# One block layer on one core: pool half of the output projection spread into the attention, residual by way of DRAM, sums of squares on VectorE, mask of the maxima on TensorE

## The chip, the cores and the metric

The kernel runs on one core of a Trainium2 chip. The metric is the device time of one execution in microseconds. The kernel before takes 1159.4 us, the median of three runs (1159.33 to 1159.95). The engines are called as in the profile: PE (TensorE) with PEld for its weight loads, DVE (VectorE), ACT (ScalarE), POOL (GpSimd), and SP (SyncE), which issues most of the transfers; ACTq and SPq are the sequencers of those engines.

## The reference, cut to what matters

```python
def _layer(h, ...):                     # h: 16 meta tokens, then 1024 frames; 1024 channels
    n1 = _rmsnorm(h, norm1_w)
    q, k, v, fg, u = split(n1 @ w_in)   # 512, 512, 512, 8, 512
    q, k = _rmsnorm per head of 64      # 8 heads
    log_f = log_sigmoid(fg + b_fgate)
    a_out = _forgetting_attention(q, k, v, cumsum(log_f))
    pooled[g] = trailing mean of u[g] over 2, 4, 8, 16 rows, minus u[g]
    p_out = (pooled @ w_pool) * pool_scale
    h = h + concat([a_out, p_out]) @ w_out
    n2 = _rmsnorm(h, norm2_w)
    return h + (silu(n2 @ w_gate) * (n2 @ w_up)) @ w_down
```

The logit of query t and key s is q_t.k_s / 8 plus the sum of log f over s < j <= t, for s <= t; the softmax runs over s. All is float32, and the 16 meta rows are dropped at the end.

## The kernel before, in words

Everything lies transposed, with channels on the partitions. A float32 product is made of three matmuls: each operand is split into a high part of type fp32r and the remainder (xh and xl, wh and wl), and high x high, high x low and low x high are added up in PSUM. So each input needs a split, ACT writing the high part and DVE or POOL the low part, before PE can use it.

The order of the program is written out by hand, and every engine works through its own list in that order.

*Opening.* A loop over the 8 blocks of 128 channels (k) loads a block of h (xs), splits it (L187 on ACT, L188 on DVE), squares it (L200 on ACT), adds the square to sqacc (L201 on POOL), and runs 15 matmuls for the first keys and the forget gates. prep_v splits the weights of v (L157 to L160). Then comes v_mm(0), the first of nine 128-row pieces of v with 24 matmuls, and then the statistics: two kinds of small matmuls over the split of sqacc give the norm as a column and as a row (pc and qrow below stand for these; L258 to L273).

*Projections* of q, k and u follow, with the gates between the v pieces, then pool_map(g) for the four window groups (L482 to L486): pm on PE, its high part mph on ACT, its low part mpl on DVE.

*Output projection.* Its work is cut into jobs in the queue fill_q: out_job(x, b) is one block of 128 output channels (m) and one half of the sequence (b), either of the pool half (12 matmuls; 16 such jobs, open at once) or of the attention's heads 0 to 3 (6 matmuls; 16 jobs, open when head 3 is done). c_job does the same for heads 4 to 7 at the end. fill(n) runs the next n of them. The residual tile h2[m] is loaded from hT once and stays in SBUF; each job adds its PSUM result into it on DVE (L552).

*Attention.* stack(h) builds the operands of a head: ACT copies the high parts, SP moves them to the other half of the partitions (K<-K and Q<-Q, L598 to L605), and DVE makes the low parts (L609, L613); background(n) takes n pieces of this. For each of the 16 units (head h, half b) a first pass computes scores and their row maxima: mx_steps does two matmuls into a tile s, and DVE reduces it (L665), or, in the last chunk of each row, adds the causal mask maskB and reduces in one instruction (L662). mt turns the maxima into rows: DVE negates and splits them (L678, L679), its inner function fin has PE transpose them in four pieces and ACT copies the rows into Q2 (L684, L685). The second pass, sp_steps, computes the scores again with the maxima as two more rows of the contraction (st, L716 to L719: K1 with Q1, the mask, K2[:68] with Q2[:68]), takes the exponential on ACT, the low part pl on POOL or DVE (L736), and multiplies with v (pv). The maxima of later units are interleaved. FILL[u] is the share of a job that a step of unit u adds; whenever the sum passes one, a job from fill_q runs.

*Tail.* The norm before the feed-forward part, gate and up, and down, which are nearly all matmuls.

## Time and profile before

| | |
|---|---|
| median of three runs | 1159.4 us |
| the profiled execution | 1160.96 us, of which the span of its instructions is 1158.5 us |
| PE busy | 1120.6 us, 97% of the span |
| DVE, ACT, POOL busy | 762.3, 485.9 and 406.7 us |
| mean granted TensorE clock | 0.989 of full speed |
| chain of work that ended last | PE 80%, DVE 12%, ACT 3%, waiting for issue 3% |

The span runs from the first instruction to the last; 2.5 us of the execution lie outside it. Busy shares are means over stages that are bound by different things, so the groups of rows further down are cut by stage. A granted clock of 1.00 is 2.4 GHz, and 0.50 is 1.2 GHz.

### The profile page before, as it was taken

What the parts mean: (1) busy time and instruction counts of PE and PEld (TensorE: products, weight loads), DVE (VectorE), ACT (ScalarE), POOL (GpSimd) and SP (SyncE); (2) the same over time, 40 slices, a digit from 0 to 9 for tenths busy, and PEclk for the clock granted to TensorE, in tenths of its full rate; (3) what the DMA queues carried; (4) which work ended last, traced back from release to release, by engine and by line L of the source; (5) the groups of instructions that cost most, each with busy time, mean ns of one, the idle gap of its engine ahead of it and who ended that gap; (6) DMA issues with size and microseconds to landing.
All of it is one profiled execution on the core that took longest, in us unless ns stands there. A gap on an engine that the chain in (4) does not pass through costs nothing.

```text
span 1158.5 us, 14614 instructions
## 1 busy us (share of the span) xinstructions
PE 1120.6 (97%) x5251; PEld 921.4 (80%) x5251; DVE 762.3 (66%) x1230; ACT 485.9 (42%) x907; POOL 406.7 (35%) x336
## 2 busy tenths in 40 slices
PE   6899999999999999998999999999999999999998
PEld 5687999877868878776788888888888888888886
DVE  7524763685778886799654554455545569778985
ACT  7333431451768776534332332233123335343541
POOL 6200235251444665638544345334533510000000
PEclk9899999999999999999999999999999999999999
DMA  6201110251012113230323132213221379542452
GB/s 222 74 1 41 50 55 11 65 162 49 20 30 48 29 38 120 109 109 1 109 73 102 44 109 73 95 51 109 73 81 65 129 261 372 189 157 100 153 193 109
DMA packets 48407, 112.45 MB, mean 97 GB/s; under 512 B 6560, under 2 KB 9120, under 8 KB 48336
## 3 DMA queue, kind: packets, MB, share of 16 engines
q1 hardware_dynamic: 38512, 95.23, 25.3%
q10 hardware_dynamic: 9824, 16.30, 3.8%
q8 instruction: 41, 0.67, 0.2%
q14 instruction: 30, 0.25, 0.1%
HBM read 86.10 MB, written 19.92 MB: 92 GB/s over the span
## 4 chain that ended last, share of the span: by engine, by line
PE 80%; DVE 12%; ACT 3%; issue 3%; POOL 1%; DMA 0%; SPq 0%; ACTq 0%; DVEq 0%; POOLq 0%
PE gu L1125 11%; PE gu L1124 11%; PE gu L1123 10%; PE d L1365 6%; PE d L1364 6%; PE d L1363 6%; PE pj L402 3%; PE pj L403 3%; PE pj L401 3%; PE o L500 2%; PE o L501 2%; PE o L502 2%; PE v L240 2%; PE v L241 1%; PE v L242 1%
## 5 line engine op out<-in xcount | busy, mean ns | idle before, releaser
L1124 PE MATMUL gu<-cb,ws 128*128 128x512 f32 x560 | 221.3, 395 | 4.2 <-DVE ws L1114 4.1
L1125 PE MATMUL gu<-cb,ws 128*128 128x512 f32 x560 | 221.1, 395 | 0.0
L1123 PE MATMUL gu<-cb,ws 128*128 128x512 f32 x560 | 220.7, 394 | 0.0
L1114 DVE TENSOR_TENSOR ws<-wst,ws 128x512 fp32r<-128x512 f32 x120 | 97.2, 810 | 125.2 <-ACT ws L1113 125.2
L1124 PEld LDWEIGHTS gu<-cb,ws 128*128 128x128 f32 x560 | 105.5, 188 | 30.0 <-DVE ws L1114 5.1
L1113 ACT ACTIVATE ws<-wst 128x512 fp32r<-128x512 f32 x120 | 70.0, 621 | 137.7 <-POOL wst L1108 130.1
L1125 PEld LDWEIGHTS gu<-cb,ws 128*128 128x128 f32 x560 | 105.7, 189 | 24.4
L1123 PEld LDWEIGHTS gu<-cb,ws 128*128 128x128 f32 x560 | 105.4, 188 | 24.6
L1365 PE MATMUL d<-hd,wd 128*128 128x512 f32 x308 | 121.2, 394 | 0.0
L1364 PE MATMUL d<-hd,wd 128*128 128x512 f32 x308 | 121.2, 393 | 0.0
L1363 PE MATMUL d<-hd,wd 128*128 128x512 f32 x308 | 121.0, 393 | 0.0
L1137 POOL TENSOR_TENSOR e<-e,e 128x512 f32<-128x512 f32 x20 | 29.6, 1479 | 158.8 <-DVE e L1150 105.7
L736 POOL TENSOR_TENSOR pl<-p,ph 128x512 fp32r<-128x512 f32 (+4 forms) x58 | 64.6, 1126 | 47.2 <-ACT p L728 45.1
L402 PE MATMUL pj<-xh,wl 128*128 128x346 f32 (+2 forms) x216 | 72.9, 338 | 0.0
L401 PE MATMUL pj<-xh,wh 128*128 128x346 f32 (+2 forms) x216 | 72.9, 337 | 0.0
L403 PE MATMUL pj<-xl,wh 128*128 128x346 f32 (+2 forms) x216 | 72.9, 337 | 0.0
L1363 PEld LDWEIGHTS d<-hd,wd 128*128 128x128 f32 x308 | 57.9, 188 | 13.4
L1364 PEld LDWEIGHTS d<-hd,wd 128*128 128x128 f32 x308 | 57.9, 188 | 13.4
L1365 PEld LDWEIGHTS d<-hd,wd 128*128 128x128 f32 x308 | 57.8, 188 | 13.2
L293 POOL TENSOR_TENSOR s<-t,g 128x346 f32<-128x346 f32 (+2 forms) x20 | 21.6, 1084 | 131.8 <-ACT g L292 124.6
L1052 ACT ACTIVATE hd<-wst 128x512 fp32r<-128x512 f32 x77 | 48.0, 623 | 35.7 <-issue 26.9
L1053 DVE TENSOR_TENSOR hd<-wst,hd 128x512 fp32r<-128x512 f32 x77 | 52.7, 685 | 9.7 <-ACT hd L1052 9.7
(292 smaller groups left out, 2560.0 us busy)
## 6 DMA issues: line engine op xcount, KB each, us to landing
wst<-in_w_d SPq DMA_DIRECT2D x77, 256.0 KB, 3.1
wst<-in_w_g SPq DMA_DIRECT2D x22, 512.0 KB, 5.2
wst<-in_w_up SPq DMA_DIRECT2D x22, 512.0 KB, 3.7
wst<-hidd SPq DMA_DIRECT2D x22, 512.0 KB, 7.5
wst<-in_w_d SPq DMA_DIRECT2D x11, 512.0 KB, 4.5
hidd<-e ACTq DMA_DIRECT2D x20, 256.0 KB
h<-in_hT SPq DMA_DIRECT2D x8, 512.0 KB, 7.8
h2d<-h SPq DMA_DIRECT2D x16, 256.0 KB, 2.0
```

The costliest lines, as they stand in the source:

```text
L401: mm(p[:, :n], wh[:, W], xh[k][:, o:o + n], start=k == 0, stop=False)
L402: mm(p[:, :n], wl[:, W], xh[k][:, o:o + n], start=False, stop=False)
L403: mm(p[:, :n], wh[:, W], xl[k][:, o:o + n], start=False, stop=k == KT - 1)
L736: sub.tensor_tensor(pl[:sz, o0:o1], p32[:sz, o0:o1], f(ph)[:sz, o0:o1], op=OP.subtract)
L1113: A.activation(t[:, :512], src, AF.Copy)
L1114: E.tensor_tensor(t[:, 512:], src, f(t)[:, :512], op=OP.subtract)
L1123: mm(p, w[:, W], c[:, :512], start=k == 0, stop=False)
L1124: mm(p, w[:, Wl], c[:, :512], start=False, stop=False)
L1125: mm(p, w[:, W], c[:, 512:], start=False, stop=k == 3)
L1363: mm(p, w[:, W], h[:, LO], start=i == 0, stop=False)
L1364: mm(p, w[:, Wl], h[:, LO], start=False, stop=False)
L1365: mm(p, w[:, W], h[:, HI], start=False, stop=i == NPR - 1)
```

## The change

It does six things.

1. *Opening.* The squares are written in place over xs by ACT, one k later than before (square), and summed on DVE (sq_add): three of the sums inside the loop and four behind prep_v. POOL has no part in it. Three pieces of v stand ahead of the statistics where one did, and the gates start two pieces later.
2. *Mask of the maxima.* In the last chunk of each row PE adds the mask with one more matmul of 128 columns; DVE then does a plain reduction.
3. *Rows of maxima.* POOL negates and splits the maxima (three instructions of 128x4 per unit), PE transposes them in one piece to 8x128, ACT copies those into a small tile mr, and SP writes them into rows 66 and 67 of Q2 with two transfers.
4. *Residual.* Each job of the pool half loads its tile, and stores the result to DRAM (h2s, 8 stores of 512 KB); each job of the attention's first half loads it from there (8 loads of 512 KB).
5. *Where the jobs run.* Of the 16 pool jobs, 8 run before the first step of the second pass (RAMP = 2, then one, then five), and the rest in the units of the first heads by FILL. Before, all 16 ran there. FILL is 13/40 and 19/40 where it was 0, 11/40 and 14/40.
6. *Before the attention.* stack(0) stands ahead of pool_map, and its pieces and those of the last q norm (run_later) go between the pool groups.

```diff
 CHQ = ((16, 512), (528, 512))
 PRE = 1
 VC, VK = 640, 6
+SQ = 4
 RA, LW = 10, 4
 NB = (3, 6)
 CW, KW, SW, W1 = 2, 2, 3, 3
...
 MID = 1
 ND, DIRECT = 2, (1, 2, 3)
 AGE = 2
-FILL = [0] * 8 + [11 / 40] * 6 + [14 / 40] * 2
+RAMP = 2
+FILL = [13 / 40] * 8 + [19 / 40] * 8
 
 
 @with_exitstack
...
 
 
     table(6)
-    xh, xl = [], []
-    sqacc = None
+    xh, xl, sqs = [], [], []
+
+    def square(k):
+
+        A.activation(sqs[k], sqs[k], AF.Square)
+
+    def sq_add(k):
+        V.tensor_tensor(sqs[0], sqs[0], sqs[k], op=OP.add)
+
     wfs = const([128, KT, 16], FR, "wfs")
     fg_ps = [ps("fg") for _ in CH3]
     k0_ps = [ps("k0") for _ in CH3]
...
                 V.tensor_tensor(wfs[:, :, 8:16], wf3, f(wfs)[:, :, 0:8], op=OP.subtract)
         xh.append(h)
         xl.append(l)
+        sqs.append(xs)
         if k == 0:
             wk0_split(slice(128, 1024))
-            sqacc = ut(L, FT, "sqacc")
-            A.activation(sqacc, xs, AF.Square)
         else:
-            sq = ut(L, FT, "sq")
-            A.activation(sq, xs, AF.Square)
-            G.tensor_tensor(sqacc, sqacc, sq, op=OP.add)
+            square(k - 1)
+        if k >= 3 and k - 2 < SQ:
+            sq_add(k - 2)
         s0, s1 = k == 0, k == KT - 1
         W = slice(128 * k, 128 * k + 128)
         for c, (o, n) in enumerate(CH3):
...
 
     for i in range(KT - VK, 4):
         prep_v(i)
+    square(KT - 1)
+    for k in range(SQ, KT):
+        sq_add(k)
+    sqacc = sqs[0]
     fgT = ut(L, FT, "fgT")
     for c, (o, n) in enumerate(CH3):
         A.activation(fgT[:16, o:o + n], fg_ps[c][:16, :n], AF.Copy)
...
         sz = min(128, L - 128 * j)
         A.activation(v32[j // 2][:sz, 512 * (j % 2):512 * (j % 2) + 512], p[:sz], AF.Copy, scale=rcol[:sz, j:j + 1])
 
-    vp = v_mm(0)
+    v0, v1, vp = v_mm(0), v_mm(1), v_mm(2)
 
 
     acch, accl = split_w(sqacc, L, ut, A, V)
...
     k32[0] = ut(L, FT, "k32")
     for (o, n), p in zip(CH3, k0_ps):
         qk_evac(p, n, slice(o, o + n), kw, k32[0][:, o:o + n])
-    vn = v_mm(1)
-    v_evac(0, vp)
+    v_evac(0, v0)
+    v_evac(1, v1)
+    vn = v_mm(3)
+    v_evac(2, vp)
     vp = vn
     now, later[:] = later[:], []
     run_later(now)
...
         return load((w_u[i] if c == "u" else w_qk[2 * i + (c == "k")]).rearrange("p k f -> p (k f)"), 1024, aux)
 
     gt = gates()
-    for j in range(2, ST):
+    for j in range(4, ST):
         vn = v_mm(j)
         v_evac(j - 1, vp)
         vp = vn
-        if j % 2 == 0:
+        if j == 4:
+            now, later[:] = later[:], []
+            run_later(now)
+        if j != 8:
             next(gt, None)
-        if j == 2:
+        if j == 5:
             A.activation(rb, qrow, AF.Ln)
             A.activation(rb, rb, AF.Exp, scale=-0.5)
             rtm = ut(L, FT, "rtm")
...
             o += 128 * (k1 - k0)
         return s
 
+    h2s = [DR.tile([128, SEQ], FT, name=f"h2s{m}") for m in range(KT)]
+    hjob, hback = {}, []
+
     def h_load(x):
-        if x < len(jobs) and jobs[x][3] and h2[jobs[x][2]] is None:
-            h2[jobs[x][2]] = ut(SEQ, FT, "h2")
-            nc.sync.dma_start(h2[jobs[x][2]], hT[:, jobs[x][2], META:])
+        if x < len(jobs) and x not in hjob:
+            mix_of, ks, m, first = jobs[x]
+            hjob[x] = ut(SEQ, FT, "h2")
+            nc.sync.dma_start(hjob[x], hT[:, m, META:] if first else h2s[m])
+            if not first:
+                h2[m] = hjob[x]
+
+    def h_store():
+        for m, t in hback:
+            nc.sync.dma_start(h2s[m], t)
+        hback.clear()
 
     def out_split(s):
         n = s.shape[1]
...
                 if y < len(jobs) and y not in wo:
                     wo[y] = out_load(y)
             h_load(x)
+        else:
+            h_store()
             h_load(x + 1)
         p = out_mm(mix_of(), wo[x], b) if p is None else p
         S = slice(512 * b, 512 * b + 512)
-        V.tensor_tensor(h2[m][:, S], p, h2[m][:, S], op=OP.add)
+        V.tensor_tensor(hjob[x][:, S], p, hjob[x][:, S], op=OP.add)
         if b == 1:
             wo.pop(x)
+            if first:
+                hback.append((m, hjob[x]))
         elif x + 1 < len(jobs):
             wo[x + 1] = out_split(wo[x + 1])
 
...
 
     vd = ut(1024, FT, "vd").rearrange("p (i j c) -> p i j c", i=2, j=4)
     V.tensor_copy(vd[:, :, :, 64:128], onesf[:, None, 0:64].to_broadcast([128, 8, 64]).rearrange("p (i j) c -> p i j c", i=2))
-    Mc = [const([128, 4, 68], FR, f"Mc{i}") for i in range(2)]
-    for t in Mc:
-        G.memset(f(t), 0.0)
-        V.tensor_copy(t[:, :, 64:66], onesf[:, 0:8].rearrange("p (a e) -> p a e", e=2))
     heads = {}
 
     SE = V
...
                 def step(T=T, o=o, n=n, a=a, c=c, last=c == nch - 1):
                     p = ps("s")
                     mm(p[:, :n], Q1[:, T], K1[:, o:o + n], start=True, stop=False)
+                    if last:
+                        mm(p[:, n - 128:n], ident, maskB, start=False, stop=False)
                     mm(p[:, :n], Q2[0:66, T], K2[0:66, o:o + n], start=False, stop=True)
-                    if last:
-                        V.tensor_tensor_reduce(p[:, :n], p[:, :n], maskB[:, 512 - n:], 1.0, -3e38, OP.add, OP.max,
-                                               accum_out=mp[:, a, c:c + 1])
-                    else:
-                        V.tensor_reduce(mp[:, a, c:c + 1], p[:, :n], op=OP.max, axis=AX.X)
+                    V.tensor_reduce(mp[:, a, c:c + 1], p[:, :n], op=OP.max, axis=AX.X)
                 steps.append(step)
                 o += n
         return steps
 
-    mcount = [0]
-
     def mt(h, b):
         Q2 = heads[h][1]
-        mc = Mc[mcount[0] % 2]
-        mcount[0] += 1
-        mx = U.tile([128, 4], FT, tag="mx", bufs=3, name=nm("mx"))
+        mx, nm_, mc = [U.tile([128, c], dt, tag=s, bufs=3, name=nm(s)) for c, dt, s in ((4, FT, "mx"), (4, FT, "mn"), (8, FR, "mc"))]
         V.tensor_reduce(mx, mparts[h, b], op=OP.max, axis=AX.X)
-        V.tensor_scalar(mc[:, :, 66:67], mx[:, :, None], -1.0, None, op0=OP.mult)
-        V.scalar_tensor_tensor(mc[:, :, 67:68], mx[:, :, None], -1.0, f(mc)[:, :, 66:67], op0=OP.mult, op1=OP.subtract)
+        G.tensor_scalar(nm_, mx, -1.0, None, op0=OP.mult)
+        G.tensor_copy(mc[:, 0:4], nm_)
+        G.tensor_tensor(mc[:, 4:8], nm_, f(mc)[:, 0:4], op=OP.subtract)
 
         def fin():
             p = ps("mt")
-            for a in range(4):
-                nc.tensor.transpose(p.bitcast(FR)[:68, 128 * a:128 * a + 128], mc[:, a, :], ident)
-            A.activation(Q2[64:68, 512 * b:512 * b + 512], p[64:68], AF.Copy)
+            nc.tensor.transpose(p.bitcast(FR)[:8, :128], mc, ident)
+            mr = U.tile([8, 128], FR, tag="mr", bufs=3, name=nm("mr"))
+            A.activation(mr, p[:8, :128], AF.Copy)
+            for i in range(2):
+                nc.sync.dma_start(f(Q2)[66 + i:67 + i, 512 * b:512 * b + 512], f(mr)[4 * i:4 * i + 4])
         return fin
 
     a32 = {}
...
     wo[0] = out_split(wo0)
     h_load(0)
     wo[1] = out_load(1)
+    stack(0)
     for g in (3, 2, 1, 0):
         pool_map(g)
-    stack(0)
-    for x in range(2):
+        background(2)
+        if g in (2, 1):
+            now, later[:] = later[:], []
+            run_later(now)
+    background(99)
+    vsplit(0)
+    for x in range(RAMP):
         fill(1)
         background(3)
-        now, later[:] = later[:], []
-        run_later(now)
-    background(4)
-    vsplit(0)
-    for _ in range(7):
-        fill(1)
-        background(2)
+    background(99)
     stack(1)
     for s in mx_steps(*units[0]):
         s()
-        background(2)
+        background(1)
     fin = mt(*units[0])
-    fill(2)
+    fill(1)
+    background(99)
     fin()
 
     acc = [None, None]
```

**Order on DVE in the opening.** The names are xl (the low part of a block of h) and xs (the block, later its square; xs_121 gathers the sum). Before, from k = 2 to the first split of the weights of v:

```order
L188 SCALAR_TENSOR_TENSOR xl_181<-xs_178,n_97,xh_180 128x1040
L188 SCALAR_TENSOR_TENSOR xl_205<-xs_202,n_97,xh_204 128x1040
L188 SCALAR_TENSOR_TENSOR xl_236<-xs_233,n_97,xh_235 128x1040
L188 SCALAR_TENSOR_TENSOR xl_260<-xs_257,n_97,xh_259 128x1040
L188 SCALAR_TENSOR_TENSOR xl_284<-xs_281,n_97,xh_283 128x1040
L159 CAST wh_307<-wst_305 128x384
L160 TENSOR_TENSOR wl_308<-wst_305,wh_307 128x1024
```

After, the same stretch:

```order
L199 SCALAR_TENSOR_TENSOR xl_179<-xs_176,n_99,xh_178 128x1040
L199 SCALAR_TENSOR_TENSOR xl_201<-xs_198,n_99,xh_200 128x1040
L158 TENSOR_TENSOR xs_121<-xs_121,xs_154 128x1040
L199 SCALAR_TENSOR_TENSOR xl_231<-xs_228,n_99,xh_230 128x1040
L158 TENSOR_TENSOR xs_121<-xs_121,xs_176 128x1040
L199 SCALAR_TENSOR_TENSOR xl_254<-xs_251,n_99,xh_253 128x1040
L158 TENSOR_TENSOR xs_121<-xs_121,xs_198 128x1040
L199 SCALAR_TENSOR_TENSOR xl_277<-xs_274,n_99,xh_276 128x1040
L170 CAST wh_298<-wst_296 128x384
L171 TENSOR_TENSOR wl_299<-wst_296,wh_298 128x1024
```

Three additions have come in between the splits; the seven that POOL did in parallel (rows sqacc<-sqacc,sq of L201) are gone from its list.

**Order on DVE between pool_map and the first maxima.** mpl are the low parts of the pool groups (the last two belong to group 0), t, s, g and q the norm of the last q block, Q and K the low parts of head 0, h the addition of a job. Before:

```order
L486 SCALAR_TENSOR_TENSOR mpl_2001<-pm_2002,psc,mph_2000 128x512
L486 SCALAR_TENSOR_TENSOR mpl_2001<-pm_2008,psc,mph_2000 128x512
L552 TENSOR_TENSOR h_331_1954<-o_2018,h_331_1954 128x512
L290 SCALAR_TENSOR_TENSOR t_2048<-qrow_398,ss_2045 128x512
L290 SCALAR_TENSOR_TENSOR t_2058<-qrow_398,ss_2055 128x512
L552 TENSOR_TENSOR h_331_1954<-o_2065,h_331_1954 128x512
L609 TENSOR_TENSOR Q_354_2036<-q_124_777,Q_353_2035 64x512
L296 SCALAR_TENSOR_TENSOR s_360_2050<-s_360_2050,g_2049 128x512
L297 SCALAR_TENSOR_TENSOR g_2049<-s_360_2050,g_2049 128x512
L298 SCALAR_TENSOR_TENSOR q_300_1832<-pj_1848,qw,g_2049 128x512
L296 SCALAR_TENSOR_TENSOR s_364_2060<-s_364_2060,g_2059 128x512
L297 SCALAR_TENSOR_TENSOR g_2059<-s_364_2060,g_2059 128x512
```

After, from the third group on:

```order
L505 SCALAR_TENSOR_TENSOR mpl_2015<-pm_2016,psc,mph_2014 128x512
L505 SCALAR_TENSOR_TENSOR mpl_2015<-pm_2022,psc,mph_2014 128x512
L639 TENSOR_TENSOR Q_331_1969<-q_117_780,Q_330_1968 64x512
L310 SCALAR_TENSOR_TENSOR s_341_1999<-s_341_1999,g_1998 128x512
L311 SCALAR_TENSOR_TENSOR g_1998<-s_341_1999,g_1998 128x512
L312 SCALAR_TENSOR_TENSOR q_293_1826<-pj_1842,qw,g_1998 128x512
L310 SCALAR_TENSOR_TENSOR s_345_2009<-s_345_2009,g_2008 128x512
L311 SCALAR_TENSOR_TENSOR g_2008<-s_345_2009,g_2008 128x512
L312 SCALAR_TENSOR_TENSOR q_293_1826<-pj_1843,qw,g_2008 128x512
L505 SCALAR_TENSOR_TENSOR mpl_2038<-pm_2039,psc,mph_2037 128x512
L505 SCALAR_TENSOR_TENSOR mpl_2038<-pm_2045,psc,mph_2037 128x512
L643 TENSOR_TENSOR K_332_1970<-k_68_484,K_332_1970 64x520
```

The last two mpl have moved from ahead of the norm to behind all of its six instructions; two t (not shown) stand ahead of group 1.

**Order on SP around the operands of head 6.** Q<-kat and K<-kat fetch gate rows, K<-K and Q<-Q are the moves of stack(6), wos is a weight of an output job. Before:

```order
L514 DMA wos_3691<-in_w_out 128x256
L592 DMA Q_748_3787<-kat_642 2x1024
L593 DMA K_750_3789<-kat_642 4x1040
L598 DMA K_750_3789<-K_749_3788 64x520 x2
L605 DMA Q_747_3786<-Q_747_3786 64x512 x2
L514 DMA wos_3909<-in_w_out 128x256
```

After; h2s is a store of a residual tile, h<-h2s a load of one, and Q<-mr the two rows of maxima that unit (5, 1) needs:

```order
L533 DMA wos_3802<-in_w_out 128x256
L622 DMA Q_777_3876<-kat_665 2x1024
L623 DMA K_779_3878<-kat_665 4x1040
L628 DMA K_779_3878<-K_778_3877 64x520 x2
L550 DMA h2s_1934<-h_541_2912 128x1024
L544 DMA h_780_3886<-h2s_1928 128x1024
L635 DMA Q_776_3875<-Q_776_3875 64x512 x2
L712 DMA Q_699_3567<-mr_3916 1x4x128 x2
L533 DMA wos_3951<-in_w_out 128x256
```

The rows of unit (5, 1) are queued behind the store, the load and the moves of the head to come.

## Rows read from the trace of the kernel before

**Rows 1.** Page, busy time and share of each engine

```profile
PE 1120.6 (97%) x5251; PEld 921.4 (80%) x5251; DVE 762.3 (66%) x1230; ACT 485.9 (42%) x907; POOL 406.7 (35%) x336
```

**Rows 2.** Windows: stretch, length, busy time per engine, granted clock, DMA share, GB/s

```profile
5.80:37.50 31.70, 23.60 (x120) 17.70 (x121) 29.48 (x19) 18.86 (x21) 21.56 (x7) 0.95 0.52 185
34.60:41.00 6.40, 5.37 (x15) 4.15 (x16) 5.59 (x9) 2.71 (x5) 0.00 (x0) 0.50 0.62 184
228.00:261.30 33.30, 32.07 (x140) 25.51 (x138) 26.06 (x38) 18.29 (x37) 16.10 (x15) 1.00 0.53 160
284.70:463.50 178.80, 168.83 (x962) 139.87 (x960) 140.21 (x320) 131.06 (x292) 96.76 (x113) 0.98 0.17 46
290.30:293.60 3.30, 3.30 (x11) 2.52 (x10) 0.63 (x2) 2.57 (x7) 0.51 (x2) 0.50 0.00 0
443.90:447.20 3.30, 3.30 (x9) 2.52 (x9) 0.69 (x1) 2.87 (x6) 3.30 (x4) 0.50 0.88 288
```

**Rows 3.** Timeline of DVE in the opening: start, length, instruction

```profile
10.24 1.30 DVE L188 SCALAR_TENSOR_TENSOR xl<-xs,n,xh 128x1040 fp32r<-128x1040 f32 x1 [0.92 <-ACT xh L187]
12.26 16.28 DVE L188 SCALAR_TENSOR_TENSOR xl<-xs,n,xh 128x1040 fp32r<-128x1040 f32 x5 [0.72 <-ACT xh L187]
40.94 1.24 DVE L128 TENSOR_TENSOR wl<-sqacc,wh 128x1040 fp32r<-128x1040 f32 x1 [0.50 <-ACT wh L125]
```

**Rows 4.** Groups of POOL, 0 to 40 us: count, busy and mean, idle before

```profile
L201 POOL TENSOR_TENSOR sqacc<-sqacc,sq 128x1040 f32<-128x1040 f32 x7 | 21.6, 3080 | 8.3 <-ACT sq L200 7.8
```

**Rows 5.** Timeline of PE in the opening, around the end of the loop

```profile
25.63 0.32 PE L209 MATMUL k<-xl,wh 128*128 128x346 f32 x1
25.79 0.32 PE L210 MATMUL fg<-xl,wfs 128*16 128x346 f32 x1
...
35.63 0.66 PE L209 MATMUL k<-xl,wh 128*128 128x348 f32 x1 [4.37 <-DVE xl L188]
37.53 0.63 PE L240 MATMUL v<-wh,xh 128*128 128x512 f32 x1
```

**Rows 6.** Timeline of DVE between pool_map and attention

```profile
232.78 5.35 DVE L486 SCALAR_TENSOR_TENSOR mpl<-pm,psc,mph 128x512 fp32r<-128x512 f32 x8
...
238.67 1.28 DVE L290 SCALAR_TENSOR_TENSOR t<-qrow,ss 128x512 f32<-128x512 f32 x2
...
243.84 1.77 DVE L296 SCALAR_TENSOR_TENSOR s<-s,g 128x512 f32<-128x512 f32 x1
...
249.46 0.89 DVE L613 TENSOR_TENSOR K<-k,K 64x520 fp32r<-64x520 f32 x1
```

**Rows 7.** Timeline of PE there: one pool job of 12 matmuls, and what follows

```profile
235.06 0.40 PE L500 MATMUL o<-mph,wo 128*128 128x512 f32 x1
...
237.86 0.40 PE L287 MATMUL ss<-sqh,bones 128*128 128x512 f32 x1
```

**Rows 8.** Waits of PE in the attention: total, times, longest

```profile
PE mt L684 <- DVE Mc L679: 3.2, 2, 2.4
PE s L659 <- DVE a L775: 1.9, 2, 1.4
PE s L659 <- DMA Q<-Q: 1.4, 1, 1.4
```

**Rows 9.** Timeline of PE at unit (3, 1)

```profile
350.16 0.41 PE L684 MATMUL mt<-ident,Mc 128*68 128x128 f32 x4
350.41 0.34 PE L716 MATMUL st<-Q,K 128*128 128x272 f32 x1
350.59 0.22 PE L718 MATMUL st<-maskA,ident 128*128 128x128 f32 x1
350.65 0.34 PE L719 MATMUL st<-Q,K 68*128 68x272 f32 x1
...
352.58 0.50 PE L716 MATMUL st<-Q,K 128*128 128x512 f32 x1
```

**Rows 10.** Timeline of SP at the same place

```profile
350.91 1.10 SPq L605 DMA_DIRECT2D Q<-Q  x2
```

**Rows 11.** Timeline of ACT at the same place

```profile
351.43 0.59 ACT L685 ACTIVATE Q<-mt 4x512 fp32r<-4x512 f32 x1
```

**Rows 12.** Transfers issued in the attention: KB each, median us to landing

```profile
Q<-Q SPq DMA_DIRECT2D x12, 128.0 KB, 2.3
```

**Rows 13.** Groups of DVE and POOL in the attention

```profile
L678 DVE TENSOR_SCALAR Mc<-mx 128x4 fp32r<-128x4 f32 x15 | 8.2, 545 | 0.5
...
L736 POOL TENSOR_TENSOR pl<-p,ph 128x512 fp32r<-128x512 f32 x31 | 40.4, 1312 | 22.4 <-ACT p L728 20.5 <-PE pv L755 1.7
```

More of the change, by code (lines that the diff above doesn't have):

```diff
@@ L102, in block_kernel @@
     V.tensor_copy(maskA, maskf)
-    maskB = const([128, 512], FT, "maskB")
-    G.memset(maskB, 0.0)
-    G.affine_select(maskB[:, 384:], maskB[:, 384:], pattern=[[-1, 128]], compare_op=OP.is_ge, fill=-BIG, base=0, channel_multiplier=1)
+    maskB = const([128, 128], FR, "maskB")
+    maskg = hs(128, FT, "maskg")
+    G.memset(maskg, 0.0)
+    G.affine_select(maskg, maskg, pattern=[[-1, 128]], compare_op=OP.is_ge, fill=-BIG, base=0, channel_multiplier=1)
+    V.tensor_copy(maskB, maskg)
     sel = const([16, 8], FT, "sel")
```

## The prediction

> **What bounds the kernel now.** I read the busy times first: PE works 1120.6 of 1158.5 us [rows 1], so the whole idle time of PE is 38 us. No change that leaves its matmuls alone can win more than that and what the half clock costs. So the next view is the windows, to see where those 38 us lie. Three of the stretches that the change touches hold 19 us [rows 2]: the opening loop from 5.8 to 37.5 us (31.7 long, PE busy 23.6, idle 8.1), the ramp between pool_map and the first maxima (33.30 against 32.07, idle 1.2) and the attention (178.80 against 168.83, idle 10.0). Beside idle time there is the clock: from 34.6 to 41.0 it is granted at 0.50, and twice in the attention for 3.3 us [rows 2]. A stretch at half clock does half its work, so the first costs 3.2 us and the other two 1.65 each.
>
> What ends those waits? In the opening it is DVE. An xl takes 1.30 us by itself, but five in a row take 16.28, 3.26 each [rows 3], and these lie under POOL's seven additions of squares, 3.08 each [rows 4]. PE meanwhile needs 15 matmuls per k, which start 0.16 us apart [rows 5], 2.4 us. So PE follows DVE, and waits 4.37 us for the last xl [rows 5]. In the attention the waits are small and for several things: the largest is 3.2 us of mt for DVE's split maxima, of which 2.4 in one piece, then 1.9 for the end of a softmax and 1.4 for a Q<-Q transfer [rows 8].
>
> **Opening.** The seven additions on POOL go, and seven of about 1.24 (the nearest DVE row with two inputs of this size, L128 [rows 3]) come to DVE, three of them in the loop. In the busiest k DVE then has 1.30 + 1.24 = 2.5 us, a hair over PE's 2.4 and with slack from the k before. The loop becomes PE's: 8 x 2.4 = 19 from 5.8, and about 2 for the first block's arrival, which nothing changes, gives 27.1 for its end in place of 37.5 [rows 5]. PE then runs three pieces of v. A job of 12 matmuls of 512 columns takes 2.80 us [rows 7], so 24 take 5.6, and three end at 43.9. The sums behind prep_v are four x 1.24, and done by about 38: hidden under the second piece of v. The statistics then start at 43.9; they took 2.8 us on PE, to 47.5, where one piece of v was done. Now three are done at 46.7, plus 1.2 that I allow because the following pieces need PSUM tiles which DVE has still to read: 47.9. Two pieces ahead, less 0.4, is **-10.8**. Bounds: -12.5 without that 1.2 and with nothing lost in the loop; -8 if the last weights of v, needed at 31 and by the order fetched only when the first wl has freed its buffer, come 3 us late.
>
> **Ramp.** Here the order decides. PE has 24 pm matmuls, four ss and two jobs: 5.6 + 0.9 + 5.6 = 12.1, from 228.0 to 240.1. Before, nine jobs stood there, and so DVE's long list lay hidden under PE. Now DVE's list is what the maxima wait for. Eight mpl took 5.35 and t began at 238.67 [rows 6]; with four mpl and no addition ahead, t begins at about 235.5. From t to s it took 5.2 (ACT's and POOL's part between), and from s to the first K 5.6 [rows 6]: so s at 240.7, the last of the norm at 246.3. Only then come the two mpl of group 0 (1.3), for which the last three matmuls of the first job wait, and K, Q, K at 0.9 [rows 6]: 250.3, and 250.8 with their handovers. PE is idle for 250.8 - 240.1 = 10.7 less the 1.2 of before, 9.5. In the attention the clock stood at 0.50 for 3.3 us after the 2.4 us wait [rows 2, 8]; once here adds 1.65. A little of this, 1.1, I expect back because POOL splits fewer weights beside DVE: **+10**. Bounds: +7 if the norm's six instructions take half their time, with less of POOL's work beside them; +12.5 if two half-clock stretches come.
>
> **PE's work.** The mask adds 64 matmuls of 128 columns; the same kind in the second pass takes 0.06 us [rows 9] (350.59 to 350.65): +3.8. Three of four transposes per unit go: four took 0.25 (350.16 to 350.41 [rows 9]), so 16 x 0.17 = -2.7 remain. Sum **+1.2**; bounds +0.5 and +4, the upper if the mask takes twice as long on narrow tiles. Everything else on PE is moved, not added.
>
> **Attention.** DVE loses its two instructions per unit on the maxima (16 x about 0.55 [rows 13], and the second alike), the reading of 64 accumulators, and later three job additions: 16 us at most of 140. Eight pool jobs and three more of the other kind move in, where PE idles. That removes most of the 10 us that wait for DVE; I leave 2.
>
> But it adds a chain. The K2, Q2 matmul of a unit's first second-pass tile needs the two rows of maxima. At unit (3, 1) the transposes end at 350.4, ACT copied them at 351.43 to 352.02 [rows 11], and st of this unit starts at 352.58 and needs them 0.3 later [rows 9]: hidden. Now ACT's copy is followed by two transfers on SP, whose queue has just then the Q<-Q of the next head, two issues from 350.91 to 352.01 [rows 10]. Two more issues of 0.55 end at 353.1, and the landing follows. What a transfer of 2 KB needs no row shows. The bounds are nothing, if it goes by bytes, and 2.3, the landing of a Q<-Q of 128 KB [rows 12]; I take 2.1, near the upper end, since the nearest row is a transfer of the same queue between the same two places, and nothing in the trace shows that its time comes from its bytes. The Trainium skill (SBUF — State Buffer, section The DMA setup-cost knee) says that a transfer pays about 2 us that do not scale with its bytes. By that the rows cost what I take; by the share of the bytes they would cost nothing, and the sum would be that of the first rival. No transfer so small has a landing in this trace.
>
> So the rows land at about 355.1, and PE waits some 2 us at (3, 1). Walked in the same way: (0, 1) and (1, 1) 0.3 each, since a job that FILL puts there covers it; (2, 1) 0.9; (4, 1), the odd head with four K<-K ahead, 3; (5, 1), with a 512 KB store and load ahead in the queue, 2; (6, 1) 1.8; (7, 1), with no head to come, 0.5. Together 11. POOL's three small instructions stand behind a pl of 1.31 [rows 13] at worst, ahead of mt, where there is room. With the 2 that stay and two or three half-clock stretches (4.2) that is 17.2, against 10.0 + 3.3 = 13.3 before: **+4**. Bounds -9 (next section) and +10.
>
> The stores and loads of the residual, 8 MB, are hidden in bytes; where they cost, it is by their place in SP's queue. The tail keeps its work but for three jobs that have moved: **0**, from -2 to +1.
>
> **Sum.** -10.8 + 10 + 1.2 + 4 + 0 = +4.4. The profiled execution took 1160.96, which is 1.5 above the median of 1159.4; the sum is a difference, so I put it on the median: 1163.8, say **1164**.
>
> **The rivals.** *The rows are covered.* If a small transfer lands at once, or the interleaved maxima of later units give PE work at each unit's front, the new waits fall to 2 and the clock is not lost: attention 4 against 13.3, -9, and the sum is -8.6: **1151**. For it speaks that PE's list alternates two passes, and that in (1, 1) and (0, 1) I find cover; against, that at (3, 1) st stands first. It decides at a sum of row waits of about 6 us, below which the kernel is faster. *The ramp is covered.* If DVE's norm runs 4 to 5 us quicker without POOL beside it, the maxima start at 246, and the gain and the losses cancel: **1159**. Against it: half of its time is a chain through ACT and POOL. *SP stands still.* SP issues in order, and a wos whose buffer PE must free is ahead of rows at (5, 1) and (6, 1). If these two units wait 4 us more each: **1172**. *The opening gives half.* The additions still meet something on DVE, or the weights of v are late, -5 in place of -10.8: **1170**.
>
> **How the numbers follow.** Forecast 0.38, rows covered 0.33, ramp covered 0.12, SP still 0.11, opening half 0.06. About 0.2% is what a measurement of this kernel can tell from no change. Faster is the first rival, 0.33; same is the second and a little of the forecast's lower edge, 0.13; slower the rest, 0.54. The forecast's own range is 1159 to 1169. For 8 in 10 the range must take in the first rival and the SP one: 1150 to 1172.
>
> **What would show it.** In the profile after: no POOL addition before 40 us, xl near 1.3 each, v at about 27; PE idle some 10 us between 215 and 245 (all is 11 earlier there), ended by DVE mpl and K; mt no longer waiting for DVE; and in the attention st waiting for the transfer of rows Q<-mr, about 1 to 3 us in units (2, 1) to (6, 1). The forecast is wrong if PE's waits for Q<-mr sum to under 6 us, if the idle stretch ahead of the first maxima is under 6, or if v starts after 31.

## The result and the profile after

The changed kernel takes 1189.7 us (median of four runs, 1186.24 to 1193.76) against 1159.68: a ratio of 1.0259 (95% interval 1.0226 to 1.0292), 30 us slower. The forecast was 1164, its range ended at 1172. The direction was right; the size was not.

The windows of the changed kernel, cut at the same places of the program as below (start, first v, first projection, pool_map, first maxima, first st, last pv, first gate-and-up matmul, end):

```profile
0.00:27.70 27.70, 21.54 (x120) 17.25 (x121) 19.73 (x29) 20.34 (x23) 2.36 (x14) 1.00 0.72 241
27.70:89.40 61.70, 60.81 (x280) 47.37 (x278) 28.83 (x59) 21.30 (x39) 3.01 (x3) 0.94 0.12 39
89.40:220.80 131.40, 130.69 (x727) 121.25 (x726) 71.86 (x106) 45.29 (x77) 39.46 (x25) 1.00 0.12 39
220.80:243.90 23.10, 15.00 (x54) 10.63 (x53) 18.17 (x28) 15.53 (x33) 8.41 (x10) 0.85 0.40 104
243.90:265.20 21.30, 21.30 (x105) 18.00 (x104) 12.82 (x24) 1.42 (x3) 4.80 (x6) 1.00 0.50 174
265.20:497.50 232.30, 212.52 (x1101) 176.07 (x1099) 132.14 (x245) 128.67 (x298) 109.36 (x163) 0.93 0.25 75
497.50:527.10 29.60, 24.58 (x93) 18.95 (x92) 23.02 (x30) 16.46 (x29) 17.43 (x13) 0.88 0.30 112
527.10:1187.90 660.80, 650.02 (x2799) 526.24 (x2798) 431.13 (x622) 231.53 (x408) 206.36 (x142) 1.00 0.36 121
```

The table below sets these beside the kernel before (its attention is in [rows 2]). Moved work is taken out: 84 output matmuls fewer ahead of the maxima, 12 fewer up to the first st, 126 more in the attention and 30 fewer behind it, each 0.233 us (2.80 for 12, [rows 7]). Lost to the clock is busy time x (1 - granted clock), summed over windows of 1 us.

| stretch | before | after | change less moved work | idle before, after | lost to the clock before, after |
|---|---|---|---|---|---|
| to the first v | 37.5 | 27.7 | -9.8 | 13.9, 6.2 | 1.0, 0.0 |
| v and statistics | 59.0 | 61.7 | +2.7 | 0.0, 0.9 | 1.8, 3.3 |
| projections | 131.5 | 131.4 | -0.1 | 0.7, 0.7 | 0, 0 |
| pool_map to maxima | 33.1 | 23.1 | +9.6 | 1.2, 8.1 | 0, 1.7 |
| maxima to first st | 23.6 | 21.3 | +0.5 | 0, 0 | 0, 0 |
| attention | 178.8 | 232.3 | +24.1 | 10.0, 19.8 | 3.4, 16.0 |
| to gate and up | 33.1 | 29.6 | +3.5 | 2.4, 5.0 | 1.7, 3.0 |
| the rest | 661.9 | 660.8 | -1.1 | 9.7, 10.8 | 3.1, 1.6 |

Over the whole execution idle time grew by 13.5 us, the loss to the clock by 14.5, and PE's work (busy time less that loss) by 1.3. The attention, forecast at +4, took 24.1. Of these 9.8 are idle time and 12.6 the clock, and only these two were in the forecast of +4; the rest is PE's own added work. What ended PE's waits, in the view of waits (total, times, longest):

```profile
PE st L746 <- DMA Q<-mr: 15.3, 7, 3.3
PE o L521 <- DVE mpl L505: 5.0, 1, 5.0
PE n L891 <- ACT wh L129: 4.7, 1, 4.7
PE mt L708 <- POOL mc L704: 4.4, 3, 1.8
```

The waits for DVE of [rows 8] are gone, as forecast; the rows of maxima are waited for instead, and mt waits for POOL's split of them. The timeline of PE at unit (3, 1), where [rows 9] show no wait before:

```profile
357.60 0.23 PE L708 MATMUL mt<-ident,mc 128*8 128x128 f32 x1
...
359.86 0.50 PE L743 MATMUL st<-Q,K 128*128 128x512 f32 x1
362.57 0.79 PE L746 MATMUL st<-Q,K 68*128 68x512 f32 x1 [2.21 <-DMA Q<-mr]
```

And the windows behind some of these waits:

```profile
270.00:276.00 6.00, 4.69 (x11) 3.65 (x12) 0.61 (x1) 2.71 (x8) 2.85 (x5) 0.50 0.52 149
362.00:368.00 6.00, 5.43 (x14) 3.78 (x14) 2.71 (x6) 2.33 (x8) 2.14 (x6) 0.51 0.00 0
420.00:423.00 3.00, 3.00 (x13) 2.74 (x12) 1.67 (x5) 2.50 (x10) 2.20 (x4) 0.52 0.00 0
478.00:481.00 3.00, 3.00 (x8) 2.25 (x9) 1.69 (x3) 1.50 (x3) 1.72 (x3) 0.52 0.88 273
```

PE is busy in nearly all of these at a granted clock of 0.50: seven such stretches lie in the attention, where there were two [rows 2]. The wait of 2.2 us that ends at 362.57 has 6 us at half clock behind it, in which 3.2 us are lost, more than the wait. Not every wait brings a stretch, and not every stretch stands behind a wait for the rows. Five of the seven do; the first, from 270, has a wait of mt for POOL ahead of it and one for the rows at its front; the one from 348 has only mt's wait for POOL. The longest of mt's three waits is followed by none:

```profile
268.36 0.22 PE L708 MATMUL mt<-ident,mc 128*8 128x128 f32 x1 [1.18 <-POOL mc L704]
346.69 0.22 PE L708 MATMUL mt<-ident,mc 128*8 128x128 f32 x1 [1.44 <-POOL mc L704]
400.84 0.22 PE L708 MATMUL mt<-ident,mc 128*8 128x128 f32 x1 [1.80 <-POOL mc L704]
```

### The profile page after: what moved, and what is told of

The parts are those of the page before. It is cut to its first block, busy times and chain, and to the rows that moved or that the text cites. A ratio compares the mean times of both kernels' runs of the same rounds, so it can differ in the third digit from the quotient of the medians.

```text
span 1187.9 us, 14672 instructions
## 1 busy us (share of the span) xinstructions
PE 1136.5 (96%) x5267; PEld 935.8 (79%) x5267; DVE 737.7 (62%) x1140; ACT 480.6 (40%) x907; POOL 391.2 (33%) x375
## 4 chain that ended last, share of the span: by engine, by line
PE 51%; DVE 5%; ACT 1%; issue 1%; POOL 0%; ACTq 0%; DVEq 0%; POOLq 0%
PE gu L1153 11%; PE gu L1152 11%; PE gu L1151 11%; PE d L1393 6%; PE d L1391 6%; PE d L1392 6%; DVE cb L913 1%; DVE h L907 1%; DVE h L1229 0%; DVE T L1231 0%; DVE w L1124 0%; DVE h L866 0%; DVE r L147 0%; ACT cb L912 0%; DVE wl L132 0%
## 5 line engine op out<-in xcount | busy, mean ns | idle before, releaser
L1165 POOL TENSOR_TENSOR e<-e,e 128x512 f32<-128x512 f32 x20 | 29.6, 1479 | 158.3 <-DVE e L1178 105.7
L693 DVE TENSOR_REDUCE mp<-s 128x1 f32<-128x144 f32 (+6 forms) x112 | 53.0, 505 | 35.7 <-PE s L692 33.9
L754 ACT ACTIVATE ph<-st 128x512 fp32r<-128x512 f32 (+4 forms) x76 | 39.2, 516 | 68.6 <-PE st L746 65.9
```

## The experiments

Theory 1: the chain that brings the rows to Q2 by DMA is the loss, each wait costing itself and a stretch at half clock. Rival A: the clock falls for other reasons. Rival B: moved jobs and residual transfers starve PE, whatever brings the rows. Theory 2, on the ramp: the maxima wait for DVE's whole list. Each median stands beside a median of the kernel before between 1159.7 and 1160.0 from the same chip.

**a_rows_act**: the changed kernel, rows as before.

```diff
-            nc.tensor.transpose(p.bitcast(FR)[:8, :128], mc, ident)
...
+            for a in range(4):
+                nc.tensor.transpose(p.bitcast(FR)[:68, 128 * a:128 * a + 128], mc[:, a, :], ident)
+            A.activation(Q2[64:68, 512 * b:512 * b + 512], p[64:68], AF.Copy)
```

> The changed kernel with only part 3 undone: DVE negates and splits the maxima, PE transposes them in four pieces, ACT copies the rows straight into Q2; no transfer of rows. Theory 1 (the chain of rows by DMA is the loss, and each of its waits also costs a stretch at half clock): the 15.3 us of waits for Q<-mr and the 4.4 for POOL's mc go, and with them 7 or so half-clock stretches of 1.7 each; 1189.7 - 15 - 11 = about 1163 (1158 to 1168), attention idle under 8, clock about 0.986. Rival A (a wait costs only itself, the clock falls for other reasons): 1174. Rival B (the moved jobs and residual transfers starve PE anyway, the waits come back under other names): over 1180.

Measured: 1167.9 us, ratio 1.0073 (1.0057 to 1.009). Its attention:

```profile
265.90:477.70 211.80, 205.33 (x1145) 172.97 (x1144) 138.74 (x275) 134.73 (x298) 100.86 (x118) 0.97 0.28 81
```

Idle falls from 19.8 to 6.5 and the clock's loss from 16.0 to 6.8: 22 us off the whole, for a part that saved PE 48 small matmuls. Rival A (1174) and rival B (over 1180) fall as they were put. The clock lost is above its expectation: three stretches remain. What is left of the loss against the opening alone (d_open), 17.9 us, belongs to the other parts and is taken apart below.

**w_busy_wait**: the changed kernel, with work for PE in the waits.

```diff
+                for _ in range(8 if j == 0 and b == 1 and h not in (1, 2) else 0):
+                    mm(p[:sz, o:o + n], K1[:, T], Q1[:, F], start=True, stop=True)
                 mm(p[:sz, o:o + n], K1[:, T], Q1[:, F], start=True, stop=False)
```

> The changed kernel with eight more matmuls of 512 columns (K1 with Q1 again, 1.87 us at full clock, their result overwritten) at the front of the second-half units of heads 0 and 3 to 7, ahead of the K2, Q2 matmul that waits for the rows. The transfers, their queue and their landing stay as they are; PE only has something to do while it waits. Theory 1 (a wait costs twice: itself, and the half-clock stretch behind it): idle in the attention falls from 19.8 by about 10, which brings nothing by itself, but the clock lost there falls from 16 to about 5; 1176 to 1181. Rival A (the clock falls for other reasons): 1188 to 1193.

Measured: 1179.71 us, ratio 1.0173 (1.0158 to 1.0188). Waits and attention:

```profile
PE st L748 <- DMA Q<-mr: 4.8, 5, 1.6
```

```profile
265.40:487.70 222.30, 213.03 (x1148) 177.38 (x1147) 132.11 (x245) 128.46 (x298) 110.10 (x163) 0.98 0.27 79
```

The 48 extra matmuls are 11.2 us of work in place of 10.5 us of idle time, so they bring nothing by themselves; the clock's loss falls from 16.0 to 5.0, and the kernel is 10.0 us faster for doing more. The five stretches at the units (3, 1) to (7, 1), 9.8 us of the loss, are gone, and the first of the seven costs 1.0 less. Of the waits left as they were, the 1.44 for POOL has lost its stretch (3.4) and the 1.80 has gained one (3.3). That decides between theory 1 and rival A: the clock fell behind the waits for the rows, and that cost about as much again as the waits themselves.

**b_rows_actq**: the row transfers on ACT's queue.

```diff
-                nc.sync.dma_start(f(Q2)[66 + i:67 + i, 512 * b:512 * b + 512], f(mr)[4 * i:4 * i + 4])
+                A.dma_start(f(Q2)[66 + i:67 + i, 512 * b:512 * b + 512], f(mr)[4 * i:4 * i + 4])
```

> The changed kernel with the two row transfers issued from ACT's queue right behind ACT's copy, not from SP's. Theory 1a (the chain itself is too long wherever it is issued: transpose, copy, two issues, landing took 2.95 us at unit (0, 1) with nothing ahead on SP): only what stood ahead on SP at (2, 1) to (6, 1) is won, 0.5 to 1.3 us each, 4 in all, and ACT loses 1.2 us per unit of issuing; 1184 to 1188. Rival (SP's order is the cause): waits for Q<-mr under 5, the clock back, 1172 or less.

Measured: 1192.44 us, ratio 1.0275 (1.0253 to 1.0297): no gain, which neither foresaw. At units (3, 1) to (6, 1) the waits are shorter by 0.4 to 1.1 (2.21 to 1.14 at (3, 1)), what SP's order had cost there. At (7, 1) the wait grows from 2.38 to 7.17: with the rows out of its queue, SP goes on to 2 MB of weights for gate and up, which it issues from 470.14 to 473.35, and ACT issues the rows just after them, at 474.53.

```profile
474.53 1.22 ACTq L712 DMA_DIRECT2D Q<-mr  x2
```

```profile
480.33 0.76 PE L746 MATMUL st<-Q,K 68*128 68x512 f32 x1 [7.17 <-DMA Q<-mr]
```

```profile
476.00:478.00 2.00, 0.00 (x0) 0.00 (x0) 0.00 (x0) 1.94 (x4) 1.76 (x2) 0.70 1.01 408
478.00:480.00 2.00, 0.00 (x0) 0.00 (x0) 1.79 (x3) 0.10 (x1) 0.00 (x0) 0.50 0.96 389
```

The DMA engines are full (share 1.01 and 0.96), and PE goes on 4.6 us behind the end of the second issue, where the changed kernel took 1.2 at this unit. So the chain is too long on either queue.

**h_one_row**: both rows in one transfer.

```diff
-            for i in range(2):
-                nc.sync.dma_start(f(Q2)[66 + i:67 + i, 512 * b:512 * b + 512], f(mr)[4 * i:4 * i + 4])
+            nc.sync.dma_start(f(Q2)[66:68, 512 * b:512 * b + 512], f(mr))
```

> The changed kernel with both rows of maxima in one transfer in place of two. Theory 1a (the chain is transpose, copy, issue and landing in a row): one issue of 0.6 less in each of the seven waits, 15.3 falls to about 11, some clock with it: 1182 to 1186. Rival (the landing alone counts, whatever is issued): no change, 1188 to 1192.

Measured: 1184.91 us, ratio 1.0208 (1.0172 to 1.0243). The waits for Q<-mr fall from 15.3 to 11.5, as theory 1a had it:

```profile
PE st L745 <- DMA Q<-mr: 11.5, 7, 2.9
```

At unit (0, 1) the chain from mt to st takes 2.44 in place of 2.95. The clock's part did not come: the loss in the attention is 16.3, against 16.0 in the changed kernel, so shorter waits brought as much half clock. The interval overlaps that of the change.

**c_split_dve**: the maxima split on DVE.

```diff
-        G.tensor_scalar(nm_, mx, -1.0, None, op0=OP.mult)
-        G.tensor_copy(mc[:, 0:4], nm_)
-        G.tensor_tensor(mc[:, 4:8], nm_, f(mc)[:, 0:4], op=OP.subtract)
+        V.tensor_scalar(mc[:, 0:4], mx, -1.0, None, op0=OP.mult)
+        V.scalar_tensor_tensor(mc[:, 4:8], mx, -1.0, f(mc)[:, 0:4], op0=OP.mult, op1=OP.subtract)
```

> The changed kernel with the maxima negated and split by DVE (two instructions, as before the change) in place of POOL's three; one transpose and the transfers of rows stay. Theory 1: the 4.4 us that mt waits for POOL turn into the 2.5 to 3.2 that it waits for DVE, and the chain of the transfers stays: 1184 to 1190, Q<-mr waits 14 to 18. Rival (POOL's queue is what makes the rows late): Q<-mr waits under 10, 1178 or less.

Measured: 1183.89 us, ratio 1.0213 (1.0176 to 1.025), an interval that overlaps that of the change. mt waits 2.7 us for DVE in place of 4.4 for POOL, and the waits for Q<-mr stay at 14.5. POOL's place is a small part, not the cause.

```profile
PE st L745 <- DMA Q<-mr: 14.5, 7, 3.7
PE mt L707 <- DVE mc L703: 2.7, 2, 2.3
```

**d_open**: the kernel before with part 1 alone.

```diff
-            G.tensor_tensor(sqacc, sqacc, sq, op=OP.add)
+            square(k - 1)
+        if k >= 3 and k - 2 < SQ:
+            sq_add(k - 2)
...
-    vp = v_mm(0)
+    v0, v1, vp = v_mm(0), v_mm(1), v_mm(2)
```

> The kernel before with the opening alone (part 1). Forecast of the prediction: -10.8, 1148.9. What the changed kernel's trace shows up to the first projection: 96.5 to 89.4, -7.1, so 1152.5 if nothing later gives it back (1151 to 1154). Rival (the earlier start is lost at the next wait, for POOL, weights or DVE): 1157 to 1160.

Measured: 1150.05 us, ratio 0.9912 (0.9897 to 0.9926). 10.0 us, better than I read from the changed kernel's trace. In the profiled execution the first projection starts 8.4 us earlier than before (96.5 to 88.1), 1.3 earlier than in the changed kernel: the stretch at half clock behind 48 us, which costs 1.6 there, is not in this execution. The rest lies in the attention, shorter by 2.7, though part 1 does not touch it; one of its two stretches at half clock is missing.

```profile
88.08 0.39 PE L417 MATMUL pj<-xh,wh 128*128 128x512 f32 x1
```

```profile
276.10:452.20 176.10, 167.36 (x962) 138.65 (x961) 141.91 (x320) 130.97 (x292) 95.83 (x113) 0.99 0.18 47
```

**f_open_mask** and **g_resid_mask**: parts 1 and 2, then parts 1, 2 and 4.

```diff
+                    if last:
+                        mm(p[:, n - 128:n], ident, maskB, start=False, stop=False)
```

> The kernel before with the opening and the mask on TensorE (parts 1 and 2), against the opening alone, 1150.05. By the rows: 64 x 0.06 = 3.8 more on PE; DVE loses 64 accumulator reads. If DVE's relief hides nothing: 1153 to 1154. Rival (attention waits for DVE fall from 8.8 to 5 or less): 1148 to 1150.

> The kernel before with parts 1, 2 and 4 (opening, mask on TensorE, residual by way of DRAM); rows by ACT and jobs where they were. Against parts 1 and 2 alone, 1153.78, it tells what the residual's stores and loads cost. If they are hidden, as the prediction had it: 1153 to 1155. Rival (they stand ahead of K<-K and Q<-Q in SP's queue, or of the weights): 1157 or more, with waits for Q<-Q or wo.

Measured: 1153.78 us, ratio 0.9951 (0.9935 to 0.9968): +3.7, the time of the first expectation but not by its sum. Against d_open's profiled execution PE's work grew by 5.4 us (0.08 for each of the 64), the loss to the clock by 3.0, and idle time fell by 4.7: DVE's relief did hide something, as the rival's condition had it. Then 1162.39 us, ratio 1.0024 (1.0011 to 1.0037): the residual's way through DRAM costs 8.6 us. Its rival is right. The attention of both:

```profile
277.10:455.90 178.80, 174.04 (x1020) 147.02 (x1018) 135.35 (x262) 131.50 (x292) 96.72 (x113) 0.98 0.18 46
```

```profile
280.40:465.60 185.20, 176.59 (x1020) 149.03 (x1019) 133.00 (x262) 131.81 (x293) 98.06 (x113) 0.96 0.24 67
```

Idle time there rises from 4.8 to 8.6 and the loss to the clock from 3.4 to 5.9. SP and PE in g_resid_mask, ahead of head 6's first maxima:

```profile
390.14 0.57 SPq L549 DMA_DIRECT2D h2s<-h  x1
390.80 0.40 SPq L543 DMA_DIRECT2D h<-h2s  x1
392.03 1.11 SPq L638 DMA_DIRECT2D Q<-Q  x2
```

```profile
399.04 0.46 PE L692 MATMUL s<-K,Q 128*128 128x144 f32 x1 [3.82 <-DMA Q<-Q]
```

A Q<-Q landed within 2.3 us before [rows 12]. Behind a store and a load of 512 KB its second issue ends at 393.14 and PE goes on at 399.04, 5.9 us later; the share of the DMA engines from 392 to 398 is 0.82 to 1.07.

**e_jobs_old**: the changed kernel without parts 5 and 6.

```diff
-RAMP = 2
-FILL = [13 / 40] * 8 + [19 / 40] * 8
+FILL = [0] * 8 + [11 / 40] * 6 + [14 / 40] * 2
...
```

> The changed kernel with parts 5 and 6 undone: all 16 pool jobs ahead of the second pass and the old order around pool_map; rows by DMA, mask on TensorE, residual by way of DRAM stay. Theory 1: the ramp's 9.6 us come back, the row waits stay and lose the cover of the pool jobs in heads 0 to 2 (16 to 20 in all, with as many half-clock stretches): 1176 to 1184. Rival B (the moved jobs are the loss in the attention): 1152 to 1160.

Measured: 1185.44 us, ratio 1.0222 (1.0194 to 1.025). The stretch from pool_map to the maxima is back to 32.9; the waits for Q<-mr rise from 15.3 to 19.0, with 16.0 lost to the clock. Theory 1 foresaw this, though the time is 1.4 above its range; rival B falls. The wait of the norm in the tail, 4.7 in the changed kernel, is short again:

```profile
PE st L745 <- DMA Q<-mr: 19.0, 8, 3.9
PE n L889 <- ACT wh L128: 1.5, 1, 1.5
```

**k1_hoist** and **k2_hoist6**: a_rows_act with all mpl ahead of the last q norm, then also six jobs.

```diff
         background(2)
-        if g in (2, 1):
-            now, later[:] = later[:], []
-            run_later(now)
+    for _ in range(2):
+        now, later[:] = later[:], []
+        run_later(now)
...
-RAMP = 2
+RAMP = 6
```

> The changed kernel with the rows by ACT (as a_rows_act, 1167.9) and the last q norm behind all four pool groups, so that DVE makes all mpl first; two jobs ahead of the maxima as now. Theory 2 (the maxima wait for DVE's whole list, and the last mpl is only where PE stands meanwhile): the first maxima start at 243 to 246 as now, PE's idle time there stays at 7 to 9, 1165 to 1169. Rival (the mpl behind the norm is the cause): idle under 3, 1158 to 1161.

> As k1_hoist with six jobs ahead of the maxima in place of two. Theory 2: four jobs of 2.8 lie where PE is idle (7 to 9) and leave the attention 11 us shorter; the ramp's loss is mostly won back: 1158 to 1162. Rival (the wait only moves into the attention, which loses the jobs that cover its waits): 1165 or more.

Measured: 1167.69 us, ratio 1.0067 (1.0052 to 1.0082), and 1166.37 us, ratio 1.0054 (1.0039 to 1.0069). In k1_hoist the wait has changed its name and not its end:

```profile
243.37 0.59 PE L693 MATMUL s<-K,Q 128*128 128x264 f32 x1 [8.14 <-DVE K L647]
```

That is theory 2. k2_hoist6 won 1.3 us of the 6 to 9 expected, and its time is the rival's. Against k1_hoist the four jobs, 11.2 us of work, lengthen the way from pool_map to the first st by 6.8, so 4.4 are won there, and the attention is only 9.7 shorter without them. The jobs in the gap wait themselves, for the split of their weights:

```profile
236.92 0.51 PE L519 MATMUL o<-mph,wo 128*128 128x512 f32 x1 [1.78 <-ACT wo L559]
239.46 0.51 PE L520 MATMUL o<-mph,wo 128*128 128x512 f32 x1 [2.04 <-POOL wo L560]
```

**z_open_hold**: d_open with one pool job held back for the first unit.

```diff
-    for _ in range(5):
+    for _ in range(4):
         fill(1)
         max_next(1)
-    max_next(2)
+    max_next(3)
...
-            share += FILL[n]
+            share += FILL[n] if n or x < 2 else 0
```

FILL[0] is 1/2 there, the other entries as before the change.

> The opening alone (1150.05) with one of the 16 pool jobs held back and run after the second step of the first unit, ahead of the transpose that waits 2.40 us for DVE there. Theory 1 (a wait costs itself and the half-clock stretch behind it, and a job in its place costs nothing): -2.4 and -1.7, 1146 (1145 to 1147). Rival (the wait only moves to the next transpose or tile): 1149 to 1151.

Measured: 1147.8 us, ratio 0.9898 (0.9867 to 0.993), the fastest version here. mt no longer waits in that unit (the 2.40 of [rows 8] is gone), and no stretch at half clock is left in the attention:

```profile
274.70:449.90 175.20, 168.45 (x974) 139.83 (x973) 140.51 (x321) 130.62 (x292) 97.84 (x113) 1.00 0.18 47
```

Its median is 2.3 below d_open's where 4 was expected; the two intervals overlap, so the medians alone do not show the gain. In the profiled executions the attention is 0.9 shorter with 2.8 us more work in it, 3.7 of the 4.1 that theory 1 gives. Its profiled execution has the stretch behind 48 us that d_open's lacks.

## Why the prediction was wrong

Put one behind the other, the versions account for the whole change: before 1159.7; opening 1150.05 (-10.0, against the kernel before of its own chip); mask 1153.78 (+3.7); residual 1162.39 (+8.6); jobs and ramp 1167.9 (+5.5); rows by DMA, split on POOL, 1189.7 (+21.8). Only the opening made the kernel faster. Two steps were measured in the other order too: the rows 23.1 (g_resid_mask to e_jobs_old), the jobs and the ramp 4.3 (e_jobs_old to the changed kernel). The residual was measured in one order, and no run has the rows by DMA without it, so how much the two cost each other is open.

- *Opening*, -10.8: right in size, -10.0, and in part by luck: up to the first projection it is 8.4 in d_open's trace and 7.1 in the changed kernel's, and the rest came from the attention, which the term did not have. xl takes 1300 ns each and the sums 1239 (nearest row 1240, [rows 3]), v starts at 27.74 for 27.1, and the allowance of 1.2 for PSUM tiles was a wait of 0.89 for DVE's qrow. Not foreseen was the clock behind that wait, nor a second stretch behind 65 us.
- *Ramp*, +10: right, +9.6. The maxima start 23.05 us behind the first pm, worked out at 22.8. The cause was right too (k1_hoist). Idle time grew by 6.9 for the 9.5 worked out; the clock took 1.7, as worked out, and the rest is PE's own work, which was put too short. *Parts 5 and 6 together* cost 5.5 with rows by ACT: against g_resid_mask's trace the ramp costs 9.9 and the tail 3.8, 4.3 come back between the first maxima and the last pv, and 1.8 elsewhere.
- *PE's work*, +1.2: right in sum, +1.3 over the whole execution. That f_open_mask took 3.7 for the mask's 3.8 is luck: its 64 matmuls are 5.4 of work, and less idle time paid for part of it.
- *Attention*, +4: this step failed, +24.1. Its sum of idle time and clock was 17.2 and measured 35.8. Two terms of it were mis-sized and one left out. The largest is the clock: "two or three half-clock stretches (4.2)" were seven, 16.0. I took their number and price from the two of before, where PE also had waits of 1.4 us that no drop followed, and did not reckon that most of the new waits would bring one. By w_busy_wait that term alone is 11 us. mt's waits for POOL, 4.4, were taken as none. The waits for rows were worked out at 11 and measured 15.3. The chain is what was described, but its landing is shorter than I took. At six of the seven units st goes on 1.1 to 1.2 us behind the end of the second issue, where I took 2.1; counted from its start, 1.8 at unit (0, 1). The Trainium skill (SBUF — State Buffer, section The DMA setup-cost knee) gives about 2 us whatever the size; counted from the start, this trace agrees. At (5, 1), with the residual's store and load ahead, it is 2.7 behind the end:

```profile
268.91 1.23 SPq L712 DMA_DIRECT2D Q<-mr  x2
414.88 1.31 SPq L712 DMA_DIRECT2D Q<-mr  x2
```

```profile
271.31 0.77 PE L746 MATMUL st<-Q,K 68*128 68x512 f32 x1 [1.40 <-DMA Q<-mr]
418.88 0.47 PE L746 MATMUL st<-Q,K 68*128 68x512 f32 x1 [3.32 <-DMA Q<-mr]
```

What was too small is the cover I counted on, 1.40 for 0.3 at (0, 1) and 2.38 for 0.5 at (7, 1), and the place beside the residual, 3.32 for 2 at (5, 1). At (3, 1) the 2.21 for 2 are two errors that cancel: there SP's issues took longer than I took, 1.90 for 1.10 and 1.31 for 1.10:

```profile
358.19 1.90 SPq L635 DMA_DIRECT2D Q<-Q  x2
360.19 1.31 SPq L712 DMA_DIRECT2D Q<-mr  x2
```

- *The residual, "hidden in bytes"*: wrong, +8.6 by g_resid_mask. I looked at its place in SP's queue and not at what a Q<-Q takes to land beside 1 MB; its sentence had no term in the sum.
- *Tail*, 0: +3.5. The norm waits 4.70 us for ACT's wh, since 30 output matmuls that lay over that chain had moved into the attention; in e_jobs_old, where they stay, it waits 1.5.
- Of the rivals none came true. "SP stands still" named two units; the wait is at seven, and b_rows_actq shows that the queue was not its core. "The rows are covered" asked for the right quantity, row waits under 6, but took a single price for it. None of the three signs of a wrong forecast appeared (row waits of 15.3, not under 6; 8.1 idle ahead of the maxima, not under 6; v at 27.7, not after 31): none of them watched the clock or the residual.

Open: why the half clock lasts 3 us behind some waits and 6 behind others, why some waits bring none, and why the one behind 48 us shows in some executions and not in others of the same opening.

## What to carry to other kernels

Where TensorE is the bound, price a new wait in front of it twice: by itself, and by a stretch of 3 to 6 us at half clock that may follow (1.5 to 3.4 us lost for each here), and look for work to put into the wait, even work that must be done anyway at another place. A row that an engine can write in place is not moved by DMA, however few its bytes, when the next matmul needs it. Large transfers put on the queue of small urgent ones delay their landing, so that bytes that fit into the idle DMA time are still not free.

## What the hardware showed that I had not expected

A wait can cost less than what follows it: 2.21 us, up to 362.57, had 6 us at a clock of 0.50, 1.2 GHz, behind it, in which 3.2 us were lost. 48 matmuls added in such waits made the kernel 10.0 us faster. The clock also stood at 0.50 from 65 to 68 us of the changed kernel with no wait ahead, behind 18 small matmuls of 2.08 us in all:

```profile
62.28 2.08 PE L338 MATMUL z<-sel,fgT 16*128 16x8 f32 x18
...
65.46 0.63 PE L255 MATMUL v<-wl,xh 128*128 128x512 f32 x1
```

d_open has the drop too; the kernel before runs the same 18 without one behind them. What brings it is not shown. And rows of 2 KB held PE for 4.6 us behind their issue where the DMA engines were full, though they came from ACT's queue and the large transfers from SP's.
